# A hybrid layer's output projection as seven block products over both sequence halves

## The chip, the core and the metric

The kernel runs on one core of one Trainium2 chip. The metric is the time of one execution in device microseconds. Before the change three runs took 1792.97, 1795.02 and 1795.41 us, so the median is 1795.02 us. The engines are called as in the profile: PE (TensorE, with PEld for its weight load), DVE (VectorE), ACT (ScalarE), POOL (GpSimd) and SP (SyncE, whose queue issues nearly all DMAs).

## What is computed

One layer over 1024 tokens of width 2048. One input projection gives the streams of two head groups. Group A is sparse attention (an indexer's scores, the best 256 keys of each query, 8 query heads and 2 key heads); group B is a chunked state-space scan (SSD). Their outputs, 1024 wide each, are put side by side, multiplied by a 2048 x 2048 matrix, added to the scaled input and normalised:

```
u = einsum('bsd,de->bse', h, w_in)
q, k, v, z_attn, q_idx, k_idx, w_idx, z_ssd, xbc, dt_raw = split(u)
...
o_attn = dsa_attention(q, k, v, q_idx, k_idx, w_idx) * silu(z_attn)
o_ssd = ssd_mixer(xbc, z_ssd, dt_raw, conv_w, conv_b, dt_bias, a_log, d_skip, norm_w)
mixed = concatenate([o_attn, o_ssd])
sub = einsum('bse,ed->bsd', mixed, w_out)
h = layer_norm(2 ** 0.25 * h + sub, ln_g, ln_b)
```

Attention is causal in chunks: queries of the first half of the sequence see keys of the first half, those of the second half see all.

## The kernel before

**Precision.** All large products are float32 split in two: a high part (rounded to the PE's float32r form) and the rest. Each product is three matmuls: high x high, high x low, low x high. So each weight block and each activation block is *split* before use: ACT writes the high part, DVE (or POOL) subtracts it to give the low part. A weight piece is 128 x 1024 floats (512 KB). It is loaded into a raw buffer (`wr`, three of them) and split into `wh` and `wl`; activations go from `u` (28 buffers of 256 KB) to `xh` and `xl` (16 each). `s4` is a pool of nine buffers of 128 x 1024 for attention, SSD and the last weight pieces.

**Stages.** The sequence is done in two halves of 512 tokens, h = 0 and 1. For each half the input projection runs over 53 tiles of 128 columns, two weight pieces each (T pieces; x stands in `xh`/`xl`). The work that depends on a tile (rotary embedding, convolution, indexer, top-k, SSD, attention) is cut into tasks whose matmuls are put between those of the projection. Then follows the output projection (O pieces): for each half, four column groups `dc` of 512, each with eight pieces of two k-tiles, and for each piece four row tiles `st` of 128 tokens; one PSUM bank gathers 16 k-tiles. The k-tiles come in the order of `E_ORDER`: first the eight of SSD, then the eight of attention. The mixed activations lie in DRAM (`mx`) between the tasks and this stage.

**What sets the order.** The program builds one fixed order of instructions for each engine. While it emits the matmuls (`run`), it keeps a model of each engine's clock and lets tasks emit a step whenever a step's inputs, buffers and engine are free in the model (`pump`, `ready`); each task has a priority, 0 first. Nothing is decided on the chip: every engine, and SP's queue, works through its list in order and waits where an input is not there. `two` picks DVE or POOL for a sum by the model's clocks. Weight pieces are loaded up to 8 and split 2 ahead of use, the last ones up to 8 ahead.

**End of the kernel.** `t_oevac` adds the scaled residual (`xn`) to a PSUM bank and takes statistics. For h = 0 the sum goes to DRAM (`h_sc`) and comes back for the layer norm (`t_ln_one`); for h = 1 it stays in `u`. The last six pieces (`SKEW`) are run row tile by row tile, so that layer norm of the last half (`t_lnstat`, `t_ln_b`) starts on row tile 0 while PE works on the others.

Of the kernel before, what the change touches and what calls it, by code (L numbers as in the profile page):

```python
# [40 lines left out]
def tile_order():  # L41
# [4 lines left out]
    for g in range(2):  # L46
# [6 lines left out]
ORDERS = [[ORDER.index(x) for x in FIRST + [y for y in ORDER if y not in FIRST]],  # L53
          [ORDER.index(x) for x in FIRST[:1] + [y for y in ORDER if y not in FIRST[:1]]]]
# [277 lines left out]
class Flow:  # L332
# [6 lines left out]
    def __init__(self, nc):  # L339
        self.sim = Sim()  # L340
        self.nc = Engines(self, nc)
        self.clk = self.sim.clk
        self.cells = []
        self.tasks = []
        self.pool = {}
        self.slots = {}
        self.where = {}
        self.n = 0
        self.idle = 0.0
        self.idles = []  # L350
        self.signals = []
# [13 lines left out]
    def avail(self, tag):  # L365
        return sum(x[0] <= self.t + 300 for x in self.slots[tag])

    def new(self, tag, shape, dtype=F):

        free = self.slots[tag]  # L370
# [150 lines left out]
class Layer:  # L521
# [20 lines left out]
    def units(self):  # L542

        pieces, work = [], []
        for h in range(2):
            tiles = ORDERS[h]
            first = len(FIRST) if h == 0 else 0
            steps = [(t, u) for u in range(2) for t in tiles[:first]]
            steps += [(t, u) for t in tiles[first:-2] for u in range(2)] + [(t, u) for u in range(2) for t in tiles[-2:]]
            for t, u in steps:  # L550
                work.append((len(pieces), None))
                pieces.append(("T", h, t, u))
        for h in range(2):
            for dc in range(4):
                for u in range(8):
                    if h == 0 or dc < 3 or u < 8 - SKEW:
                        work.append((len(pieces), (0, 1, 2, 3)))
                    pieces.append(("O", h, dc, u))
# [4 lines left out]
    def w_load(self, i):  # L563
# [3 lines left out]
        src = self.a["wt" if kind == "T" else "wo"][t, u]  # L567
        if i >= len(FIRST):
            fl.dma(raw, src)
        self.wraw[i] = raw  # L570

# [16 lines left out]

    def w_room(self):
# [10 lines left out]
    def pass_x(self, *ks):  # L600

        for k in ks:
            self.passing.add(k)
            self.fl.add(self.t_x(k), 0, f"x{k}")
# [4 lines left out]
    def t_x(self, k):  # L609
        yield Need("AV")  # L610
# [18 lines left out]
    def x_load(self, h, k):  # L629
        fl = self.fl  # L630
        raw = self.raws[k] = fl.new("u", [P, HALF])
        fl.dma(raw, self.a["xt"][h, k])

# [5 lines left out]
    def mixed_ready(self, h, k):  # L639
        e = E_ORDER[k]  # L640
        evs = [self.ev_mix[h, e]] if e >= 8 else self.ev_mix[h, e]
        return all(v.t is not None and v.t <= self.fl.t + 1500 for v in evs)

    def fetch(self, what, h, upto, need):


        fl = self.fl
        k = self.fetched
        while k < min(upto, KT):
            ok = lambda: fl.avail("u") >= (1 if k < need else 4) and (what == "x" or self.mixed_ready(h, k))  # L650
            if not ok():
                if k >= need:
                    break
                fl.drain(until=ok, why=f"{what}{h}")
            (self.x_load if what == "x" else self.mixed_load)(h, k)
# [3 lines left out]
    def run(self):  # L659
# [3 lines left out]
        self.wraw, self.w = {}, {}  # L663
        self.xh, self.xl = [None] * 16, [None] * 16
        self.raws, self.passing = {}, set()
# [4 lines left out]
        last_t = ORDERS[0][-1]  # L670
        self.fetched = 0
        for i, rows in work[2 * nf:]:
            kind, h, t, u = self.stream[i]
            edge_t = kind == "T" and t == last_t
            edge_o = kind == "O" and h == 0 and t == 3
            what = "x" if edge_t and h == 0 else "m"
            nh = 1 if (edge_t and h == 0) or edge_o else 0
            for q in range(4 if kind == "T" else len(rows)):
                fl.pump()
                if q == 0:  # L680
                    while nsp < n and nsp <= i + WAHEAD + (SKEW if self.late(nsp) else 0) and self.w_room():
# [5 lines left out]
                if kind == "T":  # L687
                    k0 = u * 8 + q * 2
                    if edge_t:
                        self.fetch(what, nh, k0 + 6, k0 + 2)  # L690
                    self.need_x(k0, k0 + 1)
                    self.emit_t(i, h, t, u, q)
                    if edge_t:
                        self.pass_x(k0, k0 + 1)
                else:
                    if edge_o and q == 0:
                        self.fetch(what, nh, 2 * u + 6, 2 * u + 2)
                    self.need_x(2 * u, 2 * u + 1)
                    self.emit_o(i, h, t, rows, u, q)
                    if edge_o and q == 3:  # L700
                        self.pass_x(2 * u, 2 * u + 1)
            if (edge_t and u == 1) or (edge_o and u == 7):
# [95 lines left out]
    def emit_o(self, i, h, dc, sts, u, q):  # L798
        fl = self.fl
        st = sts[q]  # L800
        if u == 0:
            self.wait_slots("pj", 1)
            self.pso[st] = fl.new("pj", [P, 512])
        if u == (1 if h == 1 and dc == 3 else 2) and q == 0:
            fl.add(self.t_resid(h, dc, sts), 0, f"resid{h}{dc}")
            if h == 1 and dc == 3:
                fl.add(self.t_gb(), 1, "gb")
        hi, lo = self.w[i]
        fl.await_tiles(hi, lo, *self.xh[2 * u:2 * u + 2], *self.xl[2 * u:2 * u + 2])
        for e in range(2):  # L810
            k = 2 * u + e
            mh, ml = self.xh[k][:, st * 128:(st + 1) * 128], self.xl[k][:, st * 128:(st + 1) * 128]
            wh, wl = hi[:, e * 512:(e + 1) * 512], lo[:, e * 512:(e + 1) * 512]
            fl.mm(self.pso[st], mh, wh, start=(k == 0), stop=False)
            fl.mm(self.pso[st], mh, wl, start=False, stop=False)
            fl.mm(self.pso[st], ml, wh, start=False, stop=(k == KT - 1))
        if u == 7:
            fl.add(self.t_oevac(h, dc, st, self.pso[st]), 0, f"oe{h}{dc}{st}", fl.t + 100)
# [14 lines left out]
    def consts(self):  # L833
# [5 lines left out]
        self.ps, self.pso, self.res, self.mv, self.lnB = {}, {}, {}, {}, None  # L839
# [19 lines left out]
        self.stats = self.const("stats", [P, 4, 4, 6])  # L859
# [3 lines left out]
    def start_tasks(self):  # L863
# [17 lines left out]
        self.h_sc = [[self.scratch(f"h{s}_{d}", [P, HALF]) for d in range(4)] for s in range(4)]  # L881
# [9 lines left out]
        self.tab = {}  # L891
        self.lnev = [Event() for _ in range(8)]
        self.ev_gb = Event()
        self.ev_res = {(h, dc): Event() for h in range(2) for dc in range(4)}
# [263 lines left out]
    def t_k(self, h, g, ps):  # L1158
# [7 lines left out]
        fl.free(ps, tmp)  # L1166
        yield Need()
# [51 lines left out]
    def start_attention(self, h, g):  # L1219
# [4 lines left out]
        nl = 3  # L1224
        for lane in range(nl):
            fl.add(self.t_attn(h, g, st, todo), 5, f"attn{h}{g}")

    def t_kv(self, h, g, st, total):
        fl = self.fl
        w = 512 * (h + 1)  # L1230
        if g == 1:
            yield Need(ev=(self.ev_att(h, 0),))
# [22 lines left out]
    def t_attn(self, h, g, st, todo):  # L1255
        fl, nc = self.fl, self.nc
        while todo:
            i, pr = todo.pop(0)
            n = (i + 1) * P
            q0 = i * P - h * HALF  # L1260
            heads = (2 * pr, 2 * pr + 1)
            yield Need(ev=(st["ev"], self.ev_mask[i]), u=2, s4=1 + h, keep=4)
            kv = st["kv"]
            rg = fl.new("u", [P, 2, 2, P])
            raw, gate = rg[:, 0], rg[:, 1]
            qq = fl.new("u", [P, 2, 2, P], R)
# [6 lines left out]
            src = lambda t: t[h][g][2 * pr:2 * pr + 2, :, q0:q0 + P].rearrange("r p s -> p r s")  # L1273
            fl.dma(raw, src(self.q_sc))
            fl.dma(gate, src(self.z_sc))
            yield Need("A")
# [33 lines left out]
            yield Need("P", o=1)  # L1310
            o = fl.new("o", [P, 256])
            nk = i + 1
            ahead, kb = [], 0
            while kb < nk or ahead:
                if kb < nk and len(ahead) < 3:
                    yield Need("P", a=1, u=1, now=True)
# [3 lines left out]
                    pp = fl.new("u", [P, 512], R)  # L1320
# [18 lines left out]
            yield Need()  # L1339
            for r in range(2):  # L1340
                e = 4 * g + heads[r]
                fl.dma(self.mixed[h][e][:, q0:q0 + P], gate[:, r])
                fl.signal(self.ev_mix[h, e][i - 4 * h])
            fl.free(rg)
            st["lanes"] += 1
            if st["lanes"] == 8:
                fl.signal(self.ev_att(h, g))
                if g == 1:
                    fl.free(*[self.mask[k] for k in ((2, 3) if h == 0 else (4, 5, 6, 7))])
# [60 lines left out]
    def t_ssd(self, h, g):  # L1410
# [14 lines left out]
        for cp in range(2):  # L1425
# [65 lines left out]
            yield Need("P", o=1, a=1)  # L1491
# [4 lines left out]
            o = fl.new("o", [P, 2, 2, P])  # L1496
# [214 lines left out]
```

## Time and profile before

| | |
|---|---|
| median of 3 runs | 1795.02 us |
| profiled execution, its own time | 1792.78 us |
| its span, first to last instruction | 1791.0 us |
| mean granted PE clock | 0.996 |
| HBM read and written | 204.47 MB, 32.05 MB |
| matmuls of the output projection | 1536 |
| weight loads of the output projection | 64 of 512 KB |

In the profile every instruction carries line 291, the helper through which all are emitted, so groups are told apart by tile names: `pj<-wh,xh`, `pj<-wh,xl` and `pj<-wl,xh` are the output projection (weights move, activations stand), `pj<-xh,wh` and its like the input projection, `a` and `o` the tasks' PSUM banks. A busy share of PE near 100% says that matmuls follow each other without a break; how long one takes is read from the count in a stretch. The first weight piece of the output projection is loaded at 1326.2 us.

### The profile page before, as it was taken

How to read it: one execution, taken by the hardware profiler on the slowest of the kernel's cores; microseconds unless marked ns; L12 is line 12 of the kernel's file. 1: busy time of each engine (PE TensorE's matmuls, PEld its weight loads, DVE VectorE, ACT ScalarE, POOL GpSimd, SP SyncE). 2: the span in 40 equal slices, each digit the busy share in tenths (PEclk: the TensorE clock that was granted, in tenths of full speed). 3: DMA queues.
4: the chain of work that ended last, by engine and by line, in shares of the span. 5: the costliest groups of instructions: out<-in, count | busy, mean ns of one | idle time of the engine just before them, and what ended most of it. 6: DMA issues, size and time to landing. Idle time of an engine off the chain costs nothing.

```text
span 1791.0 us, 24088 instructions
## 1 busy us (share of the span) xinstructions
PE 1763.0 (98%) x8716; PEld 1471.3 (82%) x8716; DVE 1074.6 (60%) x2136; ACT 926.3 (52%) x1570; POOL 147.9 (8%) x200
## 2 busy tenths in 40 slices
PE   9999999999999999999999999999999999999996
PEld 7888888888888877778888888888888888888885
DVE  6975666564435568887555665574656456457435
ACT  5667664442234655556788688842456344231121
POOL 0000001000001001001100010000121021010003
PEclk9999999999999999999999999999999999999998
DMA  7434333334344632122333434333336524468652
GB/s 252 131 107 118 114 112 115 115 115 132 129 147 130 203 121 69 62 70 87 106 101 115 121 112 126 116 136 129 121 108 211 163 84 127 149 210 292 202 163 95
DMA packets 118968, 238.11 MB, mean 133 GB/s; under 512 B 12736, under 2 KB 47552, under 8 KB 118848
## 3 DMA queue, kind: packets, MB, share of 16 engines
q1 hardware_dynamic: 118416, 236.18, 40.8%
q8 instruction: 68, 1.11, 0.3%
q14 instruction: 52, 0.43, 0.1%
q10 hardware_dynamic: 432, 0.39, 0.1%
HBM read 204.47 MB, written 32.05 MB: 132 GB/s over the span
## 4 chain that ended last, share of the span: by engine, by line
PE 84%; DVE 8%; ACT 5%; issue 2%; DMA 1%; POOL 0%; ACTq 0%; DVEq 0%; POOLq 0%
PE pj L291 70%; PE a L291 10%; PE o L291 4%; DVE u L291 3%; ACT u L291 3%; DVE wl L291 2%; DVE s L291 1%; ACT wh L291 1%; DVE pj L291 1%; DMA wr<-wt 1%; ACT L291 0%; ACT pj L291 0%; ACT s L291 0%; ACT a L291 0%; ACT cv L291 0%
## 5 line engine op out<-in xcount | busy, mean ns | idle before, releaser
L291 PE MATMUL pj<-xh,wh 128*128 128x512 f32 (+1 forms) x1672 | 653.4, 391 | 0.0
L291 PE MATMUL pj<-xh,wl 128*128 128x512 f32 (+1 forms) x1672 | 639.1, 382 | 0.0
L291 PE MATMUL pj<-xl,wh 128*128 128x512 f32 (+1 forms) x1672 | 638.5, 382 | 0.0
L291 DVE TENSOR_TENSOR wl<-wr,wh 128x1024 fp32r<-128x1024 f32 (+1 forms) x263 | 316.8, 1206 | 446.8 <-ACT wh L291 433.0
L291 ACT ACTIVATE wh<-wr 128x1024 fp32r<-128x1024 f32 (+1 forms) x272 | 280.9, 1034 | 268.5 <-PE pj L291 241.0
L291 PEld LDWEIGHTS pj<-xh,wl 128*128 128x128 f32 x1672 | 314.2, 188 | 62.4
L291 PEld LDWEIGHTS pj<-xh,wh 128*128 128x128 f32 x1672 | 314.6, 188 | 58.4 <-issue 2.9
L291 PEld LDWEIGHTS pj<-xl,wh 128*128 128x128 f32 x1672 | 314.8, 188 | 55.7
L291 PE MATMUL a<-u,u 128*128 128x512 f32 (+3 forms) x840 | 183.8, 341 | 5.7 <-DVE ddt L291 2.7
L291 PE MATMUL pj<-wh,xh 128*128 128x512 f32 x464 | 182.7, 394 | 0.0
L291 PE MATMUL pj<-wh,xl 128*128 128x512 f32 x464 | 180.8, 390 | 0.0
L291 PE MATMUL pj<-wl,xh 128*128 128x512 f32 x464 | 180.7, 389 | 0.0
L291 PEld LDWEIGHTS a<-u,u 128*128 128x128 f32 x840 | 136.4, 189 | 36.1 <-DVE s L291 10.5
L291 ACT ACTIVATE u<-a 128x256 fp32r<-128x256 f32 (+3 forms) x182 | 60.8, 365 | 158.0 <-PE a L291 88.4
L291 ACT ACTIVATE u<-s,sm 128x640 bf16<-128x640 int16 (+7 forms) x132 | 130.0, 985 | 10.4 <-DVE sm L291 7.9
L291 ACT ACTIVATE u<-pj 128x512 f32<-128x512 f32 x90 | 53.5, 594 | 148.1 <-PE pj L291 135.8
L291 ACT ACTIVATE a<-a 128x512 f32<-128x512 f32 (+3 forms) x160 | 75.9, 504 | 74.3 <-PE a L291 71.2
L291 PEld LDWEIGHTS pj<-wh,xl 128*128 128x128 f32 x464 | 87.1, 188 | 18.6
L291 PEld LDWEIGHTS pj<-wl,xh 128*128 128x128 f32 x464 | 87.2, 188 | 17.0
L291 PEld LDWEIGHTS pj<-wh,xh 128*128 128x128 f32 x464 | 87.2, 188 | 16.8
L291 DVE TENSOR_TENSOR u<-u,u 128x256 f32<-128x256 f32 (+8 forms) x164 | 90.3, 564 | 11.4 <-ACT u L291 10.0
L291 DVE TENSOR_TENSOR u<-a,u 128x256 fp32r<-128x256 f32 (+2 forms) x160 | 64.9, 437 | 35.5 <-ACT u L291 32.1
(120 smaller groups left out, 1662.0 us busy)
## 6 DMA issues: line engine op xcount, KB each, us to landing
wr<-wt SPq DMA_DIRECT2D x206, 512.0 KB, 3.3
wr<-wo SPq DMA_DIRECT2D x61, 512.0 KB, 3.6
u<-xt SPq DMA_DIRECT2D x32, 256.0 KB, 5.3
s<-arow SPq DMA_DIRECT2D x32, 256.0 KB, 4.3
u<-mx SPq DMA_DIRECT2D x32, 256.0 KB, 5.1
u<-xn SPq DMA_DIRECT2D x32, 256.0 KB, 5.6
out<-u SPq DMA_DIRECT2D x32, 256.0 KB, 2.8
u<-arow SPq DMA_DIRECT2D x64, 64.0 KB, 4.0
```

Source lines behind the costliest of these rows:

```text
L291: f(*args, **kw)
```

## The change

**Seven products.** With A the mixed activations in 2 x 2 blocks (rows: the two halves of the sequence; columns: the SSD and the attention half of the 2048 inputs) and B the weight matrix in 2 x 2 blocks of 1024 x 1024, the four output blocks are put together from seven products instead of eight (Strassen's scheme in Winograd's form). Sums of blocks of B (T1 to T4) are formed early and stored in DRAM (`ts`, task `t_wsum`, priority 8); sums of blocks of A (S1 to S4) are formed just ahead of each product (`t_form`, then split by `t_st`). Each product has two column groups `d` and four pieces `j`; a bank gathers eight k-tiles.

**Order of the stages.** The last eight tiles of the first half (q and z of heads 4 to 7) move behind the second half's input projection, so there are three phases and x of the first half is loaded and split again. The first half's second attention group waits for all attention of the second half. The first two products need SSD outputs only.

**Evacuation.** Products S3 and S1 are copied from PSUM by ACT; S2, A22, S4 and A12 add up to the four output blocks, with the residual prepared by `t_pre`; A11's part goes through DRAM (`pA`). The layer norm of the second half runs before the last product, that of the first half at the end. Its first two column groups now use DVE throughout, where POOL did part before. Attention tasks may also take buffers from `s4` (tag `us`) and banks from `pj` (tag `ob`), load their next inputs ahead, and store in a task of their own.

```diff
-ORDERS = [[ORDER.index(x) for x in FIRST + [y for y in ORDER if y not in FIRST]],
-          [ORDER.index(x) for x in FIRST[:1] + [y for y in ORDER if y not in FIRST[:1]]]]
+LAST = [y for y in ORDER if y[0] in ("q", "z") and y[1] >= 4]
+PHASES = [(h, [ORDER.index(x) for x in tiles]) for h, tiles in
+          ((0, FIRST + [y for y in ORDER if y not in FIRST + LAST]), (1, FIRST[:1] + [y for y in ORDER if y not in FIRST[:1]]),
+           (0, LAST))]
+ROWS = (0, 1)
+PRODUCTS = (("S3", "T3"), ("A11", "B11"), ("S1", "T1"), ("S2", "T2"), ("A22", "T4"), ("S4", "B22"), ("A12", "B21"))
...
-        for h in range(2):
-            for dc in range(4):
-                for u in range(8):
-                    if h == 0 or dc < 3 or u < 8 - SKEW:
+        for n in range(7):
+            for d in range(2):
+                for j in range(4):
+                    if n < 6 or 4 * d + j < 8 - SKEW:
                         work.append((len(pieces), (0, 1, 2, 3)))
...
+    def t_wsum(self, d, j):
+        fl = self.fl
+        yield Need("", s4=3)
+        x, y, z = [fl.new("s4", [P, 1024]) for _ in range(3)]
+        for t, name in ((x, "B12"), (y, "B11"), (z, "B22")):
+            fl.dma(t, self.w_block(name, d, j))
+        yield Need("V")
+        fl.two(y, x, y, ALU.subtract)
+        yield Need("V")
+        fl.dma(self.tsum["T1", d, j], y)
+        fl.two(x, z, x, ALU.subtract)
+        yield Need("V")
+        fl.dma(self.tsum["T3", d, j], x)
+        fl.free(x)
+        fl.two(z, z, y, ALU.subtract)
+        yield Need("")
+        fl.dma(self.tsum["T2", d, j], z)
+        fl.dma(y, self.w_block("B21", d, j))
+        yield Need("V")
+        fl.two(z, z, y, ALU.subtract)
...
+    def t_st(self, n, kk):
+        fl = self.fl
+        k = 8 * n + kk
+        yield Need("AV", ev=(self.ev_form[n, kk], *self.ev_st[max(k - 1, 0):k]), xh=1, xl=1)
+        raw = self.raws.pop((n, kk))
+        hi, lo = self.st[n, kk] = fl.new("xh", [P, HALF], R), fl.new("xl", [P, HALF], R)
+        fl.act(hi, raw)
+        fl.two(lo, raw, f32(hi), ALU.subtract)
...
+    def t_form(self, n, kk):
...
+        parts = dict(S1=("A21", "A22", "A11"), S3=("A11", "A21"), S4=("A12",)).get(name, (name,))
+        yield Need("D", ev=sum((self.mixed_ev(*blocks[b]) for b in parts), ()), us=len(parts) + 2)
+        t = []
+        for b in parts:
+            t.append(fl.new("us", [P, HALF]))
+            fl.dma(t[-1], self.mixed[blocks[b][0]][blocks[b][1]])
...
+        if name == "S3":
+            fl.two(raw, raw, t[1], ALU.subtract)
...
+        elif name == "S1":
+            fl.two(raw, raw, t[1], ALU.add)
+            fl.two(t[2], raw, t[2], ALU.subtract)
...
+        elif name == "S4":
+            x = self.s2.pop(kk)
+            fl.two(x, raw, x, ALU.subtract)
...
     def t_oevac(self, n, d, st, ps):
...
+        if name in ("S3", "S1"):
+            yield Need("A", us=1)
+            x = (self.sum_q if name == "S3" else self.sum_v)[key] = fl.new("us", [P, 512])
+            fl.act(x, ps)
...
+        elif name == "S2":
+            u, v = self.sum_u[key], self.sum_v[key]
+            x, q = t, self.sum_q.pop(key)
+            fl.tt("V", u, u, ps, ALU.add)
+            fl.free(ps)
+            fl.two(v, u, v, ALU.add)
+            fl.two(x, x, v, ALU.add)
...
+            fl.two(u, u, q, ALU.add)
...
+        else:
+            fl.tt("V", t, t, ps, ALU.subtract if name == "A22" else ALU.add)
+            fl.free(ps)
+            self.o_done(int(name == "A22"), d + (2 if name == "S4" else 0), st, t)
...
+        if (h, g) == (0, 1):
+            st["late"] = (self.ev_att(1, 1),)
...
-                eng = "V" if st and dc else "G"
+                eng = "V"
```

Two places show how the lists move. The first is SP's queue some 25 to 45 us into the program, where the first tiles of the input projection run. `wr` is a raw buffer of a T piece, `s_..<-wo` a block of the output weights for a weight sum, `ts_00` a finished sum in DRAM, `u<-ri` the rotary table. Before:

```order
L291 DMA wr_480<-wt 128x1024
L291 DMA u_522<-ri 128x512
L291 DMA u_523<-ri 128x512
L291 DMA wr_572<-wt 128x1024
L291 DMA wr_574<-wt 128x1024
L291 DMA wr_576<-wt 128x1024
L291 DMA wr_687<-wt 128x1024
```

After the change, the same place (`wr_611` holds the block that `wr_572` held):

```order
L302 DMA wr_504<-wt 128x1024
L302 DMA s_79_520<-wo 128x1024
L302 DMA s_80_521<-wo 128x1024
L302 DMA s_81_522<-wo 128x1024
L302 DMA u_552<-ri 128x512
L302 DMA u_553<-ri 128x512
L302 DMA ts_00_291<-s_80_521 128x1024
L302 DMA s_95_605<-wo 128x1024
L302 DMA s_96_606<-wo 128x1024
L302 DMA s_97_607<-wo 128x1024
L302 DMA wr_611<-wt 128x1024
L302 DMA wr_613<-wt 128x1024
```

Six loads of output weights and one store of a sum now stand ahead of the next T piece.

The second place is DVE's list from the last evacuation of a PSUM bank to the end of the program. `mv` holds the mean and scale of a row tile. Before, 15 instructions are left, the first 12 of them:

```order
L291 SCALAR_TENSOR_TENSOR u_15056<-u_15056,pj_15033 128x512
L291 BN_STATS stats<-u_15056 128x6
L291 SCALAR_TENSOR_TENSOR u_15054<-u_15054,mv_15233,u_15070 128x512
L291 SCALAR_TENSOR_TENSOR u_15054<-u_15054,mv_15233,u_15071 128x512
L291 BN_AGGR mv_15296<-stats 128x2
L291 TENSOR_SCALAR mv_15296<-mv_15296 128x1
L291 SCALAR_TENSOR_TENSOR mv_15296<-mv_15296 128x1
L291 SCALAR_TENSOR_TENSOR u_14814<-u_14814,mv_15296,u_15066 128x512
L291 SCALAR_TENSOR_TENSOR u_14814<-u_14814,mv_15296,u_15067 128x512
L291 SCALAR_TENSOR_TENSOR u_15056<-u_15056,mv_15296,u_15070 128x512
L291 SCALAR_TENSOR_TENSOR u_15056<-u_15056,mv_15296,u_15071 128x512
L291 TENSOR_TENSOR u_14527<-u_14527,u_15062 128x512
```

After, 24 are left, the first 12 of them:

```order
L302 TENSOR_TENSOR u_15387<-u_15387,pj_15531 128x512
L302 BN_STATS stats<-u_15387 128x6
L302 TENSOR_TENSOR u_15366<-u_15366,u_14771 128x512
L302 TENSOR_TENSOR u_15366<-u_15366,u_14772 128x512
L302 BN_AGGR mv_15569<-stats 128x2
L302 TENSOR_SCALAR mv_15569<-mv_15569 128x1
L302 SCALAR_TENSOR_TENSOR mv_15547<-mv_15547 128x1
L302 TENSOR_TENSOR xh_15305<-xh_15305,u_14750 128x512
L302 TENSOR_TENSOR xh_15305<-xh_15305,xl_14751 128x512
L302 SCALAR_TENSOR_TENSOR u_14961<-u_14961,mv_15547,xl_14824 128x512
L302 SCALAR_TENSOR_TENSOR u_14961<-u_14961,mv_15547,u_14825 128x512
L302 SCALAR_TENSOR_TENSOR mv_15569<-mv_15569 128x1
```

The row tile before the last (`mv_15547`) is now normalised behind the last evacuation too, with that work on DVE.

More of the change, by code (lines that the diff above doesn't have):

```diff
@@ L544, in units @@
         pieces, work = [], []
-        for h in range(2):
-            tiles = ORDERS[h]
-            first = len(FIRST) if h == 0 else 0
+        for p, (h, tiles) in enumerate(PHASES):
+            first = len(FIRST) if p == 0 else 0
             steps = [(t, u) for u in range(2) for t in tiles[:first]]
@@ L637, in mixed_load, with mixed_ev, forms @@
         fl.dma(raw, self.mixed[h][E_ORDER[k]])
[L639 to L644, printed above, removed]
+    def mixed_ev(self, h, e):
+        evs = self.ev_mix[h, e]
+        return (evs,) if isinstance(evs, Event) else tuple(evs)
+    def forms(self, n):
+        fl = self.fl
+        for kk in range(8):
+            self.passing.add((n, kk))
+            if PRODUCTS[n][0] not in ("S2", "A12"):
+                fl.add(self.t_form(n, kk), 1, f"form{n}{kk}")
+            fl.add(self.t_st(n, kk), 0, f"st{n}{kk}")
@@ L673, in run @@
             kind, h, t, u = self.stream[i]
[L674 to L677, printed above, removed]
+            edge_t = kind == "T" and rows is not None
+            what, nh = ("x", PHASES[rows + 1][0]) if edge_t and rows + 1 < len(PHASES) else ("m", ROWS[0])
             for q in range(4 if kind == "T" else len(rows)):
@@ L680, in run @@
                 if q == 0:
[L681 removed]
+                    while nsp < n and nsp <= i + WAHEAD + (SKEW if self.late(nsp) else 0) and self.w_room() and self.w_there(nsp, i):
                         self.w_split(nsp)
@@ L799, in emit_o, with bank @@
+    def bank(self, *tags):
+        fl = self.fl
+        fl.drain(until=lambda: any(fl.avail(tag) for tag in tags), why="bank")
+        return fl.new(next(tag for tag in tags if fl.avail(tag)), [P, 512])
+    def emit_o(self, i, n, d, sts, j, q):
         fl = self.fl
         st = sts[q]
[L801 to L807, printed above, removed]
+        if j == 0:
+            self.pso[d, st] = self.bank("pj", *(("a", "o") if self.ev_att(0, 1).t is not None else ()))
@@ L1309, in t_attn @@
             fl.free(sm)
-            yield Need("P", o=1)
-            o = fl.new("o", [P, 256])
+            if todo and fl.avail("us") > 4:
+                loaded = load()
+            yield Need("P", ob=1)
+            o = fl.new("ob", [P, 256])
             nk = i + 1
```

353 lines of the change are left out of this document (236 added, 117 removed).

## The prediction

> **What bounds the kernel now.** I read the page's busy line and slices first, then the table by stage, then what TensorE (PE) waited for, then the end of the chain of waits.
>
> ```profile
> span 1791.0 us, 24088 instructions
> PE 1763.0 (98%) x8716; PEld 1471.3 (82%) x8716; DVE 1074.6 (60%) x2136; ACT 926.3 (52%) x1570; POOL 147.9 (8%) x200
> ```
>
> PE is busy for 98% of the span, nothing else for more than 60%. The windows show where its 28 us of idle time lie (columns: stretch and its length; busy us and instructions of PE, weight load, VectorE (DVE), ScalarE, GpSimd (POOL); granted clock; DMA share; GB/s):
>
> ```profile
> 0.00:100.00 100.00, 96.33 (x597) 84.23 (x598) 79.16 (x145) 64.20 (x104) 3.49 (x19) 1.00 0.55 184
> 100.00:200.00 100.00, 100.00 (x468) 83.05 (x468) 60.30 (x153) 68.56 (x134) 4.94 (x15) 1.00 0.36 109
> 200.00:300.00 100.00, 100.00 (x507) 83.34 (x506) 65.45 (x150) 60.70 (x107) 7.89 (x14) 1.00 0.37 116
> ...
> 600.00:700.00 100.00, 96.67 (x459) 79.21 (x458) 69.25 (x136) 58.90 (x111) 7.99 (x13) 1.00 0.44 146
> 700.00:800.00 100.00, 99.05 (x450) 78.93 (x449) 83.50 (x138) 58.45 (x111) 3.12 (x6) 1.00 0.21 68
> ...
> 1000.00:1100.00 100.00, 98.17 (x502) 81.08 (x501) 60.49 (x137) 80.40 (x131) 12.43 (x13) 1.00 0.35 111
> ...
> 1600.00:1700.00 100.00, 100.00 (x443) 82.81 (x442) 59.07 (x79) 20.32 (x20) 4.32 (x6) 1.00 0.74 248
> 1700.00:1791.00 91.00, 73.90 (x327) 60.85 (x325) 43.83 (x61) 17.20 (x19) 19.64 (x15) 0.92 0.39 127
> ```
>
> 3.7 us go at the start and 17.1 at the end. The rest, some 7 us, lies almost all in the windows where attention runs. The end of the chain says the same: one unbroken run of matmuls, then VectorE.
>
> ```profile
> 1537.23 228.52 PE pj L291 x1008
> ```
>
> So the span is the number of matmuls times the time of one, plus 28 us. A stretch with nothing but the output projection gives that time:
>
> ```profile
> 1540.00:1770.00 230.00, 230.00 (x1016) 190.44 (x1016) 118.14 (x157) 55.30 (x62) 17.23 (x16) 1.00 0.60 198
> ```
>
> 230.00 / 1016 = **226.4 ns** from one 128x512 matmul to the next. The groups' "mean ns" of about 390 is latency that overlaps, not a price.
>
> The Trainium skill ("Trainium Kernel Development and Optimization", Best Practices) says to judge distance from the limit by LDWEIGHTS busy and not by matmul busy; by that rule PE has 18% to spare and a shorter list of matmuls would bring about 0.82 of its length. Against it stands this last row: where PE waited for nothing, its weight load is busy 190.44 of 230, 82.8%, the same share as over the whole span. For this mix 82% is full load.
>
> The same skill ("TensorE: Matmul & The Clock Gate", Wait — 56ns, not 53.3ns?) measures 215.7 ns from start to start for this width; 192 matmuls would then be an estimated 41.4 us. The row has 226.4 ns and decides.
>
> **The change, part by part.** The sum is made against the profiled execution, 1792.78 us, of which 1791.0 is span. The median of the three runs is 1795.02, 2.2 above it.
>
> *Matmuls.* Before: 2 halves x 4 column groups x 16 k-tiles x 4 row tiles x 3 = 1536. After: 7 products x 2 x 8 x 4 x 3 = 1344. The built programs agree: PE has 8012 rows before and 7820 after, 192 fewer, and all other matmuls are only moved. 192 x 226.4 ns = **-43.5 us**, all on PE's unbroken path.
>
> *Weight sums (t_wsum).* New: 8 tasks of 4 loads, 4 stores (512 KB each) and 4 subtractions of 128x1024. Their nearest price is the weight split's row.
>
> ```profile
> L291 DVE TENSOR_TENSOR wl<-wr,wh 128x1024 fp32r<-128x1024 f32 x254 | 312.6, 1231 | 442.0 <-ACT wh L291 428.2 <-DMA u<-arow 4.6 <-DMA u<-ri 3.9
> ```
>
> 32 x 1.231 = 39.4 us of VectorE, and 64 x 512 KB = 33.6 MB. By the order they stand among the first 56 weight pieces, about the first 270 us. There VectorE is busy 60 to 79% and DMA 36 to 55%; 33.6 MB over 270 us adds 124 GB/s, so some 230 to 310 GB/s. The window 1600:1700 moved 248 GB/s with PE at 100.00. So I cost steady work at nothing; its cover is PE's matmuls, and if the cover were gone it would cost VectorE's 39.4 us. What it may cost is one hold in SP's queue, near 40 us: the front part shows a store (ts) that waits for a subtraction, then three loads, ahead of wr_611. Before, the matching load went out at 29.82:
>
> ```profile
> 0.00:20.00 20.00, 18.59 (x76) 13.12 (x77) 11.42 (x19) 11.68 (x21) 1.77 (x13) 1.00 0.90 317
> 29.82 5.01 SPq L291 DMA_DIRECT2D wr<-wt  x3
> ...
> 39.49 0.40 PE L291 MATMUL pj<-xh,s 128*128 128x512 f32 x1
> ...
> 47.24 1.23 DVE L291 TENSOR_TENSOR wl<-wr,wh 128x1024 fp32r<-128x1024 f32 x1
> ...
> 48.59 0.33 PE L291 MATMUL pj<-xh,wl 128*128 128x256 f32 x1
> ```
>
> Its split ended at 48.47 and PE used it at 48.59: no slack on that side, though VectorE, not the load, was late. Now the three loads want s4 buffers that PE reads until about 39, so wr_611 goes out near 39 behind 2 MB; at the 317 GB/s of the first 20 us that has landed near 46 and is split near 48.5. Bounds 0 and 5 us (three more loads stand ahead of wr_727); I take **+2**. Nothing can be gained here.
>
> *x loaded and split twice, one stage more.* 16 more loads and splits of 256 KB. The stage changes of before lie in 600:700 and near 1331; between 1300 and 1340 PE is busy 40.00 of 40.
>
> ```profile
> 1300.00:1340.00 40.00, 40.00 (x227) 34.89 (x226) 22.56 (x62) 22.65 (x41) 6.45 (x6) 1.00 0.31 98
> ```
>
> So an edge costs about nothing; ScalarE (16 x 0.63) and VectorE (16 x 0.70) hide beside 86 us of matmuls.
>
> *Attention moved.* Three of the four groups now run beside the last eight tiles and the first two products. The 7 us of idle time of before come from such chains; I take **+1**, with -4 (all gone) and +6 (once more) as bounds.
>
> *Forms, evacuations, layer norm.* Other DMAs change by +32 loads of mixed blocks, -8 weight blocks and -16 transfers of partial sums, beside a queue that PE did not wait for at 198 GB/s; ScalarE, busy 55 of those 230 us, takes 24 evacuations and 24 more splits of 0.6 us. VectorE is what decides. From the first weight split of the fifth product to the end the order has 22 splits, 28 PSUM evacuations, 28 statistics, 48 layer-norm passes and 76 other passes of 128x512.
>
> ```profile
> L291 DVE SCALAR_TENSOR_TENSOR u<-u,pj 128x512 f32<-128x512 f32 x32 | 21.7, 678 | 19.7 <-PE pj L291 19.7
> L291 DVE BATCH_NORM_STATS2 stats<-u 128x6 f32<-128x512 f32 x32 | 22.2, 695 | 1.1
> L291 DVE SCALAR_TENSOR_TENSOR u<-u,mv,u 128x512 f32<-128x512 f32 x48 | 38.8, 829 | 8.5 <-DMA u<-h 7.4
> L291 DVE TENSOR_TENSOR xl<-u,xh 128x512 fp32r<-128x512 f32 x62 | 40.9, 698 | 22.5 <-PE pj L291 14.8 <-ACT xh L291 4.8 <-DMA u<-mx 2.6
> ```
>
> 27.1 + 19.0 + 19.5 + 39.8 + 53.0 + 3 of small ones = 161 us. PE meanwhile has 576 matmuls and two pieces of lead, 624 x 0.2264 = 141 us. So VectorE goes from half idle (118 of 230 above) to full, and the rest lies behind the last matmul. Instructions overlap a little, which lightens it: an evacuation of 0.69 is followed after 0.72 and 0.61.
>
> ```profile
> 1757.62 0.69 DVE L291 SCALAR_TENSOR_TENSOR u<-u,pj 128x512 f32<-128x512 f32 x1 [3.99 <-PE pj L291]
> 1758.34 0.69 DVE L291 BATCH_NORM_STATS2 stats<-u 128x6 f32<-128x512 f32 x1
> 1758.95 1.52 DVE L291 SCALAR_TENSOR_TENSOR u<-u,mv,u 128x512 f32<-128x512 f32 x2
> ```
>
> *Tail.* Before, the last evacuation starts at 1775.29, some 1.4 after the last matmul, with 11.5 us of VectorE to follow and 4.2 to the end of the span:
>
> ```profile
> 1773.51 0.39 PE L291 MATMUL pj<-wh,xl 128*128 128x512 f32 x1
> ...
> 1775.29 0.68 DVE L291 SCALAR_TENSOR_TENSOR u<-u,pj 128x512 f32<-128x512 f32 x1
> 1776.00 0.69 DVE L291 BATCH_NORM_STATS2 stats<-u 128x6 f32<-128x512 f32 x1
> ...
> 1779.24 4.88 DVE L291 SCALAR_TENSOR_TENSOR u<-u,mv,u 128x512 f32<-128x512 f32 x4
> 1784.03 2.73 DVE L291 TENSOR_TENSOR u<-u,u 128x512 f32<-128x512 f32 x4
> ...
> 1780.25 3.32 POOL L291 TENSOR_TENSOR u<-u,u 128x512 f32<-128x512 f32 x2 [1.12 <-ACT u L291]
> ```
>
> After, 24 instructions stand from that evacuation on: 0.7 + 0.6, ten products and sums at 0.68, eight passes at 0.76 (POOL, beside which four passes took 4.88 here, has no such work left) and 0.6 of small ones, 14.8. With 1 us of lateness and 4.2 the tail is 20.0 against 17.1: **+2.9**, bounds -1 and +11 (161 - 141 + 4.2 = 24 without any overlap, and 4 of contention).
>
> Sum: 1792.8 - 43.5 + 2 + 1 + 2.9 = 1755.2. The runs of before lie 0.2 to 2.6 above the profiled one, so I say **1756**.
>
> **The rivals.**
>
> *VectorE sets the pace of the last three products.* For it: 161 us against 141. Against it: the splits of these pieces stand early enough in the order that, adding up the rows' durations, each is done some 4 us or more before its first matmul. If half of the 48 passes take the 1.22 seen beside POOL instead of 0.76, that is 24 x 0.46 = 11 us more, and with no overlap 4 more: 1756 + 11 to 15 = 1767 to 1771.
>
> *A product waits for attention.* S1 needs the second half's last head, S4 the first half's. For it: 600:800 lost 4.3 us to such chains. Against it: the built order has 74 other DMAs between that head's last store and its load. One chain of some 10 us exposed gives 1766.
>
> *PE has room that its busy time hides.* Weight load is busy 82% of the span; if the other 18% were waits that stay when matmuls go, 0.82 x 43.5 = 35.7 us are saved and the time is 1764. Against it: the 82.8% where nothing is waited for. This is what the skill's rule on LDWEIGHTS above would give.
>
> *SP's queue holds the weights: slower.* All 32 stores of weight sums wait, in SP's one queue, for a subtraction of lowest priority, and every weight load behind them waits too, while three raw buffers are the reserve. From a mean exposed hold of (43.5 - 5.9) / 32 = 1.2 us per store the gain is gone; at 1.4 it is 1756 + 45 = 1801. For it: the one hold found near 40 us. Against it: after the first 60 us PE's pieces take 5.4 us each at a DMA share of 0.36.
>
> That the change does not do what it says is excluded by the 192 rows.
>
> **How the numbers follow.** Forecast 0.70 (own range 1747 to 1763: -1 -4 +0 to 5 +6 on the terms, cut where they would all have to coincide); VectorE's pace 0.14; attention 0.07; hidden room 0.03; SP's queue 0.04; anything else near no change 0.02. Faster by over 0.2% (3.6 us, about what a measurement here can tell) 0.94, within it 0.02, slower 0.04. The range for 8 in 10: 1747 to 1772.
>
> **What would show it.** PE with 192 fewer matmuls at 226 ns; PE idle below 30 us and none of it between 1400 us and the last matmul; PE fully busy in the first 300 us but for some 2 us near 47; VectorE above 85% over the last 150 us; 19 to 22 us from the last matmul to the end. It is wrong if matmuls of the products come slower, if PE shows waits for wl or xl in the last products, or for a weight load before 270 us.

## The result and the profile after

The change takes 18.6 us off, half of what was forecast, and the time lies 3.6 us above the range's upper end of 1772.

| | before | after |
|---|---|---|
| median of 4 runs (lowest to highest), us | 1794.15 (1792.97 to 1795.41) | 1775.55 (1773.47 to 1776.51) |
| ratio to before, with its 95% interval | 1 | 0.9895 (0.9877 to 0.9912) |
| span of the profiled execution, us | 1791.0 | 1773.5 |
| last matmul ends, us from the span's start | 1773.90 | 1751.11 |
| from there to the end of the span, us | 17.1 | 22.4 |

From the page of after, the span and the busy line:

```profile
span 1773.5 us, 24039 instructions
PE 1727.7 (97%) x8524; PEld 1434.8 (81%) x8524; DVE 1180.9 (67%) x2293; ACT 944.6 (53%) x1616; POOL 151.2 (9%) x195
```

PE has 8716 - 8524 = 192 matmuls fewer, as counted. But its idle time, 28.0 us before, is 1773.5 - 1727.7 = 45.8 us now. The table by stage of after says where (columns as in the prediction; the last row is a stretch of products in which PE waits for nothing):

```profile
0.00:100.00 100.00, 98.13 (x602) 85.11 (x603) 80.57 (x144) 62.39 (x98) 4.24 (x20) 1.00 0.70 244
...
40.00:60.00 20.00, 20.00 (x166) 19.86 (x165) 19.02 (x36) 13.56 (x19) 1.30 (x4) 1.00 0.85 325
...
830.00:1050.00 220.00, 214.10 (x1070) 176.67 (x1069) 127.67 (x292) 178.54 (x297) 14.08 (x16) 1.00 0.37 116
...
1250.00:1550.00 300.00, 292.03 (x1506) 244.92 (x1505) 183.06 (x400) 151.99 (x291) 38.88 (x44) 1.00 0.52 169
...
1339.00:1402.00 63.00, 55.78 (x286) 45.80 (x287) 38.39 (x90) 32.69 (x60) 6.91 (x8) 1.00 0.48 159
1402.00:1550.00 148.00, 147.48 (x780) 125.14 (x780) 88.37 (x197) 72.98 (x155) 22.55 (x28) 1.00 0.56 180
...
1600.00:1751.00 151.00, 147.98 (x648) 120.84 (x646) 137.96 (x205) 41.05 (x50) 9.98 (x8) 1.00 0.59 188
...
1604.00:1659.00 55.00, 55.00 (x243) 45.22 (x243) 48.61 (x70) 15.94 (x20) 2.40 (x1) 1.00 0.63 208
```

The stretch that was unbroken before now has holes. The same 300 us of before:

```profile
1250.00:1550.00 300.00, 299.96 (x1598) 257.10 (x1597) 170.31 (x400) 135.57 (x258) 45.91 (x39) 1.00 0.40 129
```

Eight us are lost there, 7.2 of them between 1339 and 1402. This is PE's timeline in the worst part of it (start, busy us, engine, line, operation, names and shapes, count, and in brackets the idle time ahead of it and what ended that):

```profile
1387.31 0.39 PE L302 MATMUL pj<-wl,xh 128*128 128x512 f32 x1
1387.53 0.39 PE L302 MATMUL pj<-wh,xl 128*128 128x512 f32 x1
1389.15 0.92 PE L302 MATMUL a<-c,s 128*128 128x128 f32 x4 [1.23 <-DVE sm L302]
1389.82 0.65 PE L302 MATMUL pj<-u,u 128*128 128x256 f32 x3
...
1393.75 0.79 PE L302 MATMUL a<-u,xh 128*128 128x384 f32 x3 [0.56 <-DVE sm L302]
1395.20 1.50 PE L302 MATMUL a<-u,xh 128*128 128x512 f32 x6 [0.66 <-DVE sm L302]
1396.91 0.41 PE L302 MATMUL a<-c,s 128*128 128x128 f32 x2 [0.22 <-DVE sm L302]
1397.08 1.10 PE L302 MATMUL pj<-xl,u 128*128 128x256 f32 x7
1399.79 0.50 PE L302 MATMUL pj<-xl,u 128*128 128x256 f32 x2 [1.60 <-DVE xl L302]
1400.80 0.50 PE L302 MATMUL pj<-wh,xh 128*128 128x512 f32 x1 [0.52 <-DVE u L302]
```

The first product (moving operand `wh` or `wl`) starts at 1383.68 and stops after 18 matmuls, three of its four row tiles with six each. Then PE has attention alone, a score or a transpose at a time with VectorE's row maximum or split in between, until the fourth row tile starts at 1400.80. The attention is that of the second half (its scores have 512 and 384 columns), and its output sums stand in `pj`, the tag of the projection's four PSUM banks.

For an account of the whole I took the start of every matmul and counted what it starts later than its predecessor's length allows (0.227 us for 512 columns, 0.173, 0.119 and 0.112 for 384, 256 and 128), wherever that is more than 0.28 us. Long waits of PE in us, by place:

| place (us of after) | before | after |
|---|---|---|
| to 300 | 2.7 | 2.6 |
| first half's attention (549 to 680) | 6.3 | 3.5 |
| second half's state-space groups (836 to 1045) | 3.0 | 6.9 |
| end of the tiles, first two products, attention beside them (1273 to 1526) | 0 | 10.2 |
| last four products (1598 to 1725) | 0 | 4.0 |
| sum | 11.9 | 27.1 |

So the matmuls bring -43.5, the long waits +15.2, the tail +5.3. The span fell by 17.5; the 5.5 that remain are waits under 0.28 us each. Counted in the same way, 3.8 of them are new between 1100 and 1600 us, 2.6 are new in the first 300 us (6.1 for 3.5), and 0.8 went from the first half's attention.

Three of the waits in the last four products end with a step of VectorE. Two, at 1661 and 1688 us, are for a PSUM bank that it has not emptied (`xh<-xh,pj`, `u<-u,pj`). The third is for a weight split (`wl`) that stands in its list behind passes of the layer norm (lines of VectorE's timeline and PE's):

```profile
1660.52 0.68 DVE L302 TENSOR_TENSOR xh<-xh,pj 128x512 f32<-128x512 f32 x1
1661.35 0.47 PE L302 MATMUL pj<-wh,xh 128*128 128x512 f32 x1 [1.32 <-DVE xh L302]
...
1723.22 0.75 DVE L302 SCALAR_TENSOR_TENSOR u<-u,mv,u 128x512 f32<-128x512 f32 x1
1723.88 1.22 DVE L302 TENSOR_TENSOR wl<-wr,wh 128x1024 fp32r<-128x1024 f32 x1
1725.16 0.50 PE L302 MATMUL pj<-wl,xh 128*128 128x512 f32 x1 [1.19 <-DVE wl L302]
```

### The profile page after: what moved, and what is told of

Same layout as the page of the kernel before. It is cut to its first block, busy times and chain, and to the rows that moved or that the text cites. A ratio compares the mean times of both kernels' runs of the same rounds, so it can differ in the third digit from the quotient of the medians.

```text
span 1773.5 us, 24039 instructions
## 1 busy us (share of the span) xinstructions
PE 1727.7 (97%) x8524; PEld 1434.8 (81%) x8524; DVE 1180.9 (67%) x2293; ACT 944.6 (53%) x1616; POOL 151.2 (9%) x195
## 5 line engine op out<-in xcount | busy, mean ns | idle before, releaser
L302 DVE TENSOR_TENSOR wl<-wr,wh 128x1024 fp32r<-128x1024 f32 (+2 forms) x251 | 301.9, 1204 | 349.1 <-ACT wh L302 347.6
L302 PE MATMUL a<-u,u 128*128 128x128 f32 (+3 forms) x804 | 180.9, 343 | 5.8 <-DVE u L302 2.4
L302 PE MATMUL pj<-wh,xh 128*128 128x512 f32 x374 | 148.2, 396 | 2.7 <-DVE xh L302 1.6
L302 PE MATMUL pj<-wl,xh 128*128 128x512 f32 x374 | 146.0, 390 | 1.2 <-DVE wl L302 1.2
L302 PE MATMUL pj<-wh,xl 128*128 128x512 f32 x374 | 145.9, 390 | 0.0
L302 DVE TENSOR_TENSOR u<-u,u 128x512 f32<-128x512 f32 (+9 forms) x191 | 109.7, 588 | 14.8 <-ACT u L302 12.9
L302 ACT ACTIVATE xh<-u 128x512 fp32r<-128x512 f32 (+1 forms) x87 | 52.3, 623 | 72.7 <-DVE u L302 29.4
L302 DVE SCALAR_TENSOR_TENSOR s<-a,wsc,s 128x512 f32<-128x512 f32 (+3 forms) x120 | 73.2, 646 | 22.6 <-ACT a L302 21.8
L302 PEld LDWEIGHTS pj<-wh,xh 128*128 128x128 f32 x374 | 70.3, 188 | 17.8 <-DVE u L302 2.1
L302 PEld LDWEIGHTS pj<-wh,xl 128*128 128x128 f32 x374 | 70.2, 188 | 15.0
```

The source lines that it names most:

```text
L302: f(*args, **kw)
```

## The experiments

Four questions: does the moved attention cost what stands beside it (A) or pay for it (B); do the weight sums cost anything early (C, D); is VectorE too full at the end (E); and is it PSUM banks (F) or something behind them (G) that holds the first products? Differences below are from 1775.55 where nothing else is said; with four runs each, two kernels whose runs overlap differ by nothing that this shows. The kernel before took 1794.15 us beside the change, 1793.10 beside the first four kernels below, 1794.64 beside the next four and 1794.83 beside the last two, so some 1 us of such a difference can come from that.

**The old tile order under the seven products.** The three stages become the two of before:

```
-          ((0, FIRST + [y for y in ORDER if y not in FIRST + LAST]), (1, FIRST[:1] + [y for y in ORDER if y not in FIRST[:1]]),
-           (0, LAST))]
+          ((0, FIRST + [y for y in ORDER if y not in FIRST]), (1, FIRST[:1] + [y for y in ORDER if y not in FIRST[:1]]))]
...
-        if (h, g) == (0, 1):
-            st["late"] = (self.ev_att(1, 1),)
```

> The seven products stay; the eight q and z tiles of the first half go back into its own stage, and the first half's second attention group runs early again, as before the change. Theory A, the move is the cost (some 9 us of long waits at 1339 to 1401 us and 4 of short ones stand beside that group now): these go, 1761 to 1766 us. Theory B, the move is the cover: beside the second half's last attention there are then only two products, 2 x 192 matmuls x 0.2264 = 87 us, in place of 174 us of output projection before the change, and the third product needs that attention's result; it waits some 25 to 30 us, 1795 to 1810 us, with the wait behind the second product. Either way the long waits of 836 to 1045 us (6.9 us now, 3.3 before the change) fall back to 3 to 4 if the move caused them.

Measured: 1806.68 us (1805.03 to 1807.19), ratio to before 1.007 (1.0053 to 1.0087). B holds and A falls. The seven products without the move are slower than the kernel before. Its table by stage, with the clock in finer rows behind it:

```profile
1400.00:1480.00 80.00, 79.97 (x386) 66.75 (x385) 42.03 (x82) 38.23 (x65) 6.46 (x8) 1.00 0.56 180
1480.00:1580.00 100.00, 74.00 (x378) 59.08 (x377) 55.25 (x136) 36.93 (x85) 14.74 (x12) 0.85 0.29 91
...
1561.00:1564.00 3.00, 1.33 (x9) 1.33 (x10) 2.32 (x4) 0.74 (x4) 0.00 (x0) 0.89 0.00 0
1564.00:1567.00 3.00, 1.82 (x9) 1.52 (x8) 0.85 (x2) 0.32 (x1) 0.00 (x0) 0.50 0.00 0
1567.00:1570.00 3.00, 0.00 (x0) 0.00 (x0) 0.00 (x0) 0.00 (x0) 0.00 (x0) 0.50 0.71 218
...
1577.00:1579.00 2.00, 2.00 (x6) 1.51 (x6) 0.59 (x1) 0.60 (x1) 0.00 (x0) 0.50 0.00 0
1579.00:1581.00 2.00, 2.00 (x8) 1.57 (x7) 0.00 (x0) 0.60 (x1) 0.00 (x0) 0.65 0.00 0
1581.00:1583.00 2.00, 2.00 (x10) 1.66 (x9) 0.00 (x0) 0.60 (x1) 0.00 (x0) 1.00 0.00 0
```

PE loses 26 us in one stretch, at the head of the third product (its first matmul is at 1481.4); counted as above, its long waits after 1300 us are 34.8 against 13.8. The granted clock falls to 0.50 in it, and matmuls of 512 columns then follow each other every 0.43 us. The state-space groups have some 5 us of waits here (6.9 with the move, 3.0 before), which decides nothing about them.

**No weight sums.** The products that take a sum take a plain weight block, and `t_wsum` is not started:

```
-            return self.tsum[name, d, j]
+            name = dict(T1="B11", T2="B12", T3="B21", T4="B22")[name]
...
-                fl.add(self.t_wsum(d, j), 8, f"wsum{d}{j}")
+                pass
```

> Left out: the weight sums; the products with a sum take a plain block of the weights, so the output is another. Theory C, the sums cost time early (VectorE's 39 us, 33.6 MB, SP's queue): 4 us or more faster, below 1771. Theory D, they lie beside matmuls as the first 300 us of the trace say (PE's long waits 2.6 us now, 2.7 before the change): within 3 us, 1772 to 1777; the start alone may give 1 to 2.

Measured: 1773.38 us (1771.51 to 1776.25). The runs overlap with those of the change: by the time, D. The traces are sharper, and they show a cost. PE's waits in the first 300 us, counted as above, long and short together, are 6.7 us without the sums and 6.2 before the change, 8.7 in the change and 7.7 to 9.6 in the nine other kernels here that have the sums: some 2 us. The start of a single matmul hides this. The 1600th matmul of the tiles starts at 395.0 us with the sums and at 395.2 without them, but with them 16 fewer of the tasks' small matmuls (1.8 us) have run by then. One place is near 105 us. VectorE with the sums and then without them:

```profile
105.00:125.00 20.00, 19.04 (x84) 15.16 (x83) 19.43 (x26) 11.64 (x18) 4.64 (x5) 1.00 0.79 262
105.00:125.00 20.00, 20.00 (x90) 16.65 (x90) 12.67 (x22) 9.63 (x14) 0.47 (x4) 1.00 0.25 88
```

In the change a weight sum (`s<-s,s`) stands in VectorE's list, followed without a gap by the steps of the task for one of which PE then waits:

```profile
104.12 1.22 DVE L302 TENSOR_TENSOR s<-s,s 128x1024 f32<-128x1024 f32 x1
...
107.21 1.86 PE L302 MATMUL a<-u,u 128*128 128x512 f32 x6 [0.96 <-DVE u L302]
```

The long waits alone hide it too (2.6 and 2.7 us): 1.8 at this place and 0.4 near 86 us are new, and those near 58 and 68 us, 2.3 in the kernel without the sums, are gone.

**No layer-norm passes for the second half's rows** (the two passes in `t_ln_one` taken out):

```
-        fl.stt(x, x, mv[:, 0:1], g, ALU.subtract, ALU.mult)
-        fl.stt(x, x, mv[:, 2:3], b, ALU.mult, ALU.add)
```

> Left out: the 32 scale-and-shift passes of 128x512 on VectorE for the second half's rows (24 us beside the last three products); the rows are stored without them. Theory E, VectorE is too full there: the waits of 4.0 us between 1598 and 1726 go, and so does its lag of 2 to 3 us behind the last matmul: 1768 to 1771. Rival, those waits stand in the order and not in VectorE's load: within 2 us, 1773 to 1777.

Measured: 1770.39 us (1767.83 to 1771.04), 5.2 less. E's time came. Of the 4.0 us of long waits in the last four products (3.1 in the trace of the new tail order below, whose lists are the same up to there) 1.7 are left, and the tail is 18.5 us. But from 1671 us on VectorE's list has another order too, and from 1683 PE's, so the load and the order are not taken apart here. VectorE in one stage (the same row of after shows 89.83):

```profile
1600.00:1700.00 100.00, 98.97 (x435) 81.12 (x434) 80.61 (x119) 32.72 (x42) 7.55 (x6) 1.00 0.70 229
```

**The projection's banks kept from attention.** In the planner, attention's sum may take one of the four `pj` banks while more than `keep` are free; `keep` goes from 2 to 4 when the first product's operands are begun:

```
-            return self.avail("o") + max(self.avail("pj") - 2, 0)
+            return self.avail("o") + max(self.avail("pj") - self.keep, 0)
...
                         self.forms(0)
+                        fl.keep = 4
```

> Attention's output sums may take a PSUM bank of the projection's four only until the first product's operands are begun; from there they have their own one. Theory F, the stretch of 1387.5 to 1400.8, in which PE has attention alone (30 short matmuls, some 8 us of waits), stands there because the first product's fourth sum has no bank: 1766 to 1769. Theory G, the attention chain itself has too little room before the third product needs it: the wait only moves to the head of that product, near 1510, and is as long; 1773 to 1780.

Measured: 1777.92 us (1777.29 to 1778.44), 2.4 more. From the table by stage of this kernel:

```profile
1380.00:1402.00 22.00, 21.75 (x100) 17.89 (x99) 15.07 (x31) 13.77 (x23) 0.00 (x0) 1.00 0.64 220
1510.00:1535.00 25.00, 18.91 (x91) 14.91 (x90) 19.41 (x46) 12.27 (x34) 7.89 (x9) 0.90 0.69 218
```

The bank was what stopped the first product: with it, the hole at 1387 is closed. But F's time did not come. A hole of 6.1 us opens at the head of the third product (first matmul at 1507.8), with the clock at 0.90 in it, as G said: long waits after 1300 us are 11.7 against 13.8, and the time is worse.

**The banks kept only for the first product's first column group.** As the last edit, and in `o_tasks`:

```
+        if (n, d, j) == (0, 1, 1):
+            fl.keep = 2
```

> As the run that kept the projection's four PSUM banks from attention's output sums, but only until the first product's first column group has them; then attention may take the free ones again. Theory G, attention's chain before the third product is the limit: part of the wait comes back at one place or the other, 3 to 7 us of long waits between 1339 and 1535 us in place of 9.5, 1770 to 1774. Theory F, the bank was the whole cost: 1766 to 1769. If the banks make no difference at all: 1775 to 1779, as in that run.

Measured: 1773.64 us (1773.01 to 1774.25), 1.9 less and within G's time, though the runs overlap with those of the change. The long waits between 1339 and 1545 us are 8.6 (2.5 at the end of the tiles, 0.7 in the first product, 5.4 in the first four of the third product's eight pieces). Up to 1535, G's window, they are 5.4, within its 3 to 7; the longest, 3.2 us, comes at 1539.

**The layer norm's order in the tail.** After the change VectorE ends like this (its timeline):

```profile
1753.62 0.69 DVE L302 TENSOR_TENSOR u<-u,pj 128x512 f32<-128x512 f32 x1 [0.28 <-issue]
...
1757.66 0.69 DVE L302 TENSOR_TENSOR xh<-xh,u 128x512 f32<-128x512 f32 x1 [0.88 <-ACT xh L302]
...
1761.48 0.69 DVE L302 TENSOR_TENSOR xh<-xh,u 128x512 f32<-128x512 f32 x1 [0.88 <-ACT xh L302]
...
1768.49 1.41 DVE L302 TENSOR_TENSOR u<-u,u 128x512 f32<-128x512 f32 x2
```

In `t_ln_b` both ScalarE steps are put first, and a column group that needs VectorE alone goes ahead of theirs:

```
-        for dc in (0, 2, 3, 1):
+        for dc in (0, 1):
+            x = self.res[0, dc, st]
+            fl.act(x, x, AF.Identity, bias=mv[:, 3:4], scale=mv[:, 2:3])
+        for dc in (2, 0, 3, 1):
...
-                fl.act(x, x, AF.Identity, bias=mv[:, 3:4], scale=mv[:, 2:3])
```

> Only the order of the last layer norm changes: ScalarE normalises both of its column groups first, and VectorE takes one of its own groups before it needs the first of them. Theory H, part of the tail of 22.4 us is order: VectorE's two waits of 0.88 us for ScalarE after the last matmul go, 1.5 to 3 us less, 1772.5 to 1774. Rival, the tail is VectorE's backlog alone: within 1 us, 1774.5 to 1776.5.

Measured: 1773.22 us (1772.04 to 1774.86), 2.3 less; the tail is 19.0 us for 22.4. Its VectorE, from the last evacuation on, waits once for GpSimd and never for ScalarE:

```profile
1755.55 0.68 DVE L302 TENSOR_TENSOR u<-u,pj 128x512 f32<-128x512 f32 x1
...
1759.42 0.16 DVE L302 SCALAR_TENSOR_TENSOR mv<-mv 128x1 f32<-128x1 f32 x1 [0.66 <-POOL mv L302]
...
1763.72 2.74 DVE L302 TENSOR_TENSOR u<-u,u 128x512 f32<-128x512 f32 x4
```

H holds in the trace, where PE's list is the same as in the change and VectorE's differs only from 1736 us on. By time it is not shown: the runs overlap.

**Both edits.**

> Both edits together. If their effects lie at different places they add: the sum of the two differences from 1775.5, within 1.5 us; by H and G 1767 to 1772.

Measured: 1771.16 us (1770.64 to 1771.76), ratio to before 0.9872 (0.9855 to 0.9888). 4.4 less than the change, and the two alone make 1.9 + 2.3 = 4.2, as if they added. No run of it overlaps with a run of the change; by its median it is the fastest kernel here that computes everything.

**Half the cover.**

```
-LAST = [y for y in ORDER if y[0] in ("q", "z") and y[1] >= 4]
+LAST = [y for y in ORDER if y[0] == "z" and y[1] >= 4]
```

> Only the four z tiles are worked late, the four q tiles go back into the first half's own stage: 43 us less of other matmuls beside the second half's attention. Theory G, the wait is what that cover lacks: long waits after 1300 us between the 10 of all eight tiles late and the 32 of none late, 18 to 24 us, and 1784 to 1794 us. Rival, the cost is one of switching stages or of the reload of x, not of cover: no more waits than now, 1774 to 1778.

Measured: 1773.74 us (1772.99 to 1775.27). G falls in this form: the long waits after 1300 us are 13.0, as with all eight tiles late, not 18 to 24. They lie elsewhere, though: none in the first product, most between 1474 and 1577. So B holds only as far as that: with none of the tiles late some 20 us of waits come on top, with four or eight late they stay at 11 to 14 whatever else was tried.

**Data or queues.** The kernel with the banks kept for the first column group, but no product reads an attention block:

```
-        e1, e2 = E_ORDER[kk], E_ORDER[8 + kk]
+        e1 = e2 = E_ORDER[kk]
```

> As the run that gave attention the free banks back (1773.6 us), with the same order on every engine, but the products read the state-space blocks in the place of attention's blocks, so no product's operand depends on attention and the output is another. Theory G1, the third product waits for attention's stored result: its long waits of 5.8 us between 1515 and 1545 us go, 1767 to 1769. Theory G2, it waits because its operands stand in the engines' queues behind attention's work: the waits stay, 1772 to 1775.

Measured: 1775.09 us (1773.67 to 1776.59). The long waits of that stretch are 5.4 us in both kernels (the 5.8 expected took in one at 1597). PE's waits from 1510 to 1545, with attention's blocks (columns: waited for, us in total, times, longest)

```profile
PE pj L302 <- ACT xh L302: 4.3, 2, 3.0
PE pj L302 <- DVE u L302: 0.6, 1, 0.6
```

stand in the view of the kernel without them as the same two lines, to the digit.

G2: the third product does not wait for attention's result here. Nor does that result set the place of its operands in the lists: in the two traces the orders of PE, VectorE, ScalarE, GpSimd and of SP's DMAs are the same, instruction by instruction, though in the second the planner had no attention to wait for. What PE does wait for is in the timelines of the run without the dependence, ScalarE and then VectorE:

```profile
1538.62 1.06 ACT L302 ACTIVATE wh<-wr 128x1024 fp32r<-128x1024 f32 x1 [1.72 <-PE pj L302]
1541.57 0.63 ACT L302 ACTIVATE xh<-xh 128x512 fp32r<-128x512 f32 x1 [1.90 <-DVE xh L302]
```

```profile
1539.71 1.23 DVE L302 TENSOR_TENSOR wl<-wr,wh 128x1024 fp32r<-128x1024 f32 x1 [1.09 <-ACT wh L302]
1540.85 0.69 DVE L302 TENSOR_TENSOR xh<-xh,u 128x512 f32<-128x512 f32 x1
1541.57 0.69 DVE L302 TENSOR_TENSOR u<-xh,u 128x512 f32<-128x512 f32 x1
```

ScalarE cannot split the next weight piece before PE is done with the `pj` matmul it waits for; VectorE stands in its queue with that piece's other half; the sums that make the third product's operand (`xh<-xh,u`) come behind it; ScalarE then splits the sum; and PE waits for that split (3.0 us). Three engines work in order here, each behind a neighbour. Why the planner put the operands so late, for want of a buffer or of engine time in its model, was not settled.

**Row statistics on ScalarE.** With the tail's new order, the second half's `bn_stats` become a sum and a sum of squares on ScalarE:

```
+        if h == 1:
+            fl.add(self.t_stat(h, dc, st, x), 1, f"stat{h}{st}", fl.clk["V"])
+            return
         self.nc.vector.bn_stats(self.stats[:, 4 * h + st, dc], x)
...
+        fl.act(self.junk, x, AF.Copy, accum_out=acc[:, dc:dc + 1])
+        fl.act(self.junk, x, AF.Square, accum_out=acc[:, 4 + dc:5 + dc])
```

> The run with the layer norm's new order (1773.2 us), and the second half's 16 row statistics of 128x512 on ScalarE (a sum and a sum of squares) in place of VectorE: 16 x 0.61 less some 2 us of small ones, about 8 us of VectorE's work gone between the fourth product and the sixth. Theory E, VectorE's load is what PE waits for there: a third of the 5.2 us that 24 us less work brought, 1770.5 to 1772. Rival, the place of single instructions decides: 1773 to 1775.

Measured: 1773.69 us (1770.09 to 1776.20), beside 1773.22 without it. The runs scatter over 6 us, so it is not told apart from either theory by time. The stage is emptier and PE no fuller (98.48 without the edit):

```profile
1600.00:1700.00 100.00, 98.21 (x432) 80.64 (x431) 83.91 (x139) 52.38 (x100) 3.59 (x4) 1.00 0.63 206
```

So some 8 us less work on VectorE brought nothing that can be measured where 24 us brought 5.2. The order changed in both kernels, so the shares of VectorE's load and of the place of single instructions stay open.

## Why the prediction was wrong, point by point

- **What bounds the kernel, and the price of a matmul: right.** 55.00 / 243 = 226.3 ns in the products, 226.4 was used; 192 fewer, -43.5 us. The rival of hidden room falls with it: the price did come off, and what ate it were waits that can be pointed at.
- **Weight sums +2 from a hold near 47 us: the size came true, by luck.** PE is busy 20.00 of 20 between 40 and 60 us, so the hold is not there. Some 2 us are lost all the same: near 105 us, where VectorE, whose steady work I had at nothing, is busy 19.43 of 20, and in short waits whose cause wasn't isolated. The slower-than-before rival, SP's queue, did not happen: the long waits up to 300 us are 2.6, 2.7 before.
- **Attention moved, +1 with bounds -4 and +6: this step failed.** The term measures about +10 (10.2 of long and 3.8 of short waits where it stands now, less 2.8 and 0.8 at the old place), above the upper bound. I priced it by the waits of attention's old place, 7 us in all. There it had the projection's banks and the queues of tiles that need little else. At the new place it shares both with products whose operands are made, split and summed by the same engines. Of this sharing the runs show the bank (the hole at 1387 closes when it is kept free) and, in the third product, the wait in a row of engines that work in order; no run touched the 2.5 us at the end of the tiles. The move itself was needed: without it the kernel takes 1806.7.
- **An edge costs about nothing: wrong at one edge.** Where the tiles end and the products begin, the fourth sum finds no bank, 1387.5 to 1400.8. Closing that hole opened another at the head of the third product.
- **A product waits for attention (rival, one chain of some 10 us): the place, not the reason.** 5.4 us of waits do stand at the head of the third product once the bank is free, and they stay when no product depends on attention. Under the old tile order, where PE has attention alone for 44 us there (1506 to 1550), this was not tried.
- **Splits done 4 us or more before their matmul: wrong.** VectorE is 91% busy from 1600 to 1751 (137.96 of 151), as forecast, and from 1598 on PE waits 4.0 us where I had 0. Only 1.2 of them are for a split; the other two long waits shown are for banks that VectorE empties late, which I had not asked after.
- **Tail +2.9: +5.3.** VectorE was late by 2.5 us at the last evacuation, not 1 (a low figure: it was 1.4 before the change), with the norm of two row tiles still to do, and waited twice 0.88 us for ScalarE. The new order alone takes 3.4 off; in the old order, leaving out the second half's passes takes 3.9 off, so the two causes overlap.
- **What I had at nothing and didn't name:** 3.9 us more of waits in the second half's state-space groups. The old tile order had some 5 of the 6.9; their cause wasn't isolated.

The misses together: +9.4 attention (10.4 for 1), +4.0 last products, +2.4 tail, +3.9 state-space groups, 19.7. The two profiled executions differ by 17.5 in span where -43.5 + 2 + 1 + 2.9 = -37.6 was forecast, a miss of 20.1; by the medians it is 1775.55 - 1756 = 19.6. The forecast of 1756 added 0.8 to the sum, though the median known then lay 2.2 above the profiled run.

## What to carry to other kernels

When work is moved, price it by what it shares at the new place (banks, buffers, the queues of the engines between it and the bound one), not by what it waited at the old one. An engine that is 98% busy has its gains in instructions removed, but each hole that the removal opens costs in full, and closing one hole with a static order often only moves it: look for the next one before counting the gain. Compare two orders by the work done up to a point, not by when one instruction starts. And a wait "for" another stage should be tried without the data dependence before it is believed.

## What the runs showed of the hardware

After a stretch in which PE has little to do it runs slow for a while. In the run with the old tile order the granted clock is 0.50 from 1564 to 1579 us (the rows shown there). It had fallen ahead of the long wait of 6.27 us below, after 3 us with PE busy for 1.33. PE's timeline has this:

```profile
1572.09 0.80 PE L301 MATMUL pj<-wh,xh 128*128 128x512 f32 x1 [6.27 <-ACT xh L301]
...
1576.31 0.63 PE L301 MATMUL pj<-wl,xh 128*128 128x512 f32 x1
1576.73 0.63 PE L301 MATMUL pj<-wh,xl 128*128 128x512 f32 x1
```

Matmuls of 512 columns that wait for nothing start every 0.43 us instead of 0.227, and last 0.63 instead of 0.39. They follow one another from 1576.31 on, and the full clock is back between 1579 and 1581, some 3 to 5 us later. The Trainium skill ("TensorE: Matmul & The Clock Gate", Part 1: The HAM clock gate) has the same two states and a return after about 3.4 us of sustained work; the trace agrees. In the change itself the clock is 1.00 in the windows of its waits (830 to 1050, 1339 to 1402 and 1600 to 1751), the longest of which is 2.5 us, so they cost their own length and no more. The same wait does not always pass so: behind that of 2.4 us at 987 us the clock is 1.00 from 992 to 994 us in the change and 0.50 in the kernel that gives the banks back, with the same lists up to there.
